# Feed-forward parts of 6 plain, 8 and 8 seven-product chunks, operands made in four steps, first turn of a part outside the weight ring

## The chip, the cores and the metric

The kernel runs on one core of a Trainium2 chip. Its time is the device time of one execution in microseconds (us); lower is better. TensorE (PE) multiplies, VectorE (DVE), ScalarE (ACT) and GpSimd (POOL) do the elementwise work, and SyncE (SP) issues nearly all DMAs. Each engine takes its instructions in the order in which they stand in its queue, and an instruction that waits holds up all behind it.

## The reference

A decoder trunk of two layers on 512 tokens of width 1024, in float32. Layer 0 is a convolution module, layer 1 differential attention. After each comes a SwiGLU feed-forward block of inner width 2816, which is what this change touches, and then a gated embedding:

```
h = h + conformer_conv(rms_norm(h))          # layer 0; layer 1: diff_attention
u = rms_norm(h, ffn_norm_g)
h = h + (silu(u @ w_gate) * (u @ w_up)) @ w_down
h = h + sigmoid(rms_norm(h, ple_norm_g) @ w) * (p @ w_proj)
```

## The kernel before

Activations lie transposed: a chunk is 128 features by 512 tokens, so h is 8 chunks and the inner width 22. Every float32 factor is split in two float32r parts, hi (a cast on ACT) and lo (a subtraction on DVE), and a product is three matmuls (`mm3`, L165 to L167): lo by hi, hi by hi, hi by lo.

**Weights.** `weight()` loads a tile of 128x1024 (SP) into a ring `wraw` of two buffers, casts it into a ring `whi` of four (ACT, L158) and subtracts into a ring `wlo` of four (DVE, L160). A ring slot comes free when the last matmul that reads it has ended.

**The feed-forward block**, `ffn()`, runs in three parts of 8, 8 and 6 inner chunks. Each part makes its hidden chunks (gate, up, silu, product, split into hi and lo in B tiles) and then runs its piece of the down-projection, `linear()`: for each of 8 output chunks m, one weight tile and as many `mm3` as the part has chunks, added to h by DVE (L885). Outputs 0 and 1 are computed together.

Hidden chunks are made in two ways. **Plain:** 24 matmuls of 512 columns each for gate and for up. **Seven-product:** two chunks at once. The input and the weights are taken as 2x2 blocks and the four block products come from seven, each of 12 matmuls of 256 columns, on sums and differences of blocks. One such turn (a `Unit`: Gate, then Up) needs, for its weights, six steps of `prep`: step 0 splits A11 and A12, steps 1 and 3 form sums on POOL (L721, L722, L726, L727), step 2 splits S1 and S2, step 4 splits S3 (L730, L731), step 5 splits S4 and A22. Steps 0, 2 and 5 each take a slot of `whi` and `wlo` (`two()`, L711, L712). For its input side it needs, once a layer, the operands of `operands()`: for four pairs of chunks, two scaled chunks u (DVE, L663), B11 (L666, L667), B21 and B22 (L670, L671), four differences T1 to T4 (POOL, L675 to L678) and their split (L680, L681).

In part one, 4 chunks are plain and 4 are seven-product; parts two and three are all seven-product. `operands()` stands in the program behind plain chunk 0, and the `prep` of part one's first turn behind plain chunk 3. The first turn of a later part is loaded and prepared by `begin()`, which `linear()` calls ahead of the weight of output chunk 6 of the part before. A Unit's result of its first product leaves PSUM by an ACT copy (L754), and product 6 then accumulates into the same PSUM half.

The order on each engine is set by a scheduler at build time, which moves instructions by its own estimate of times, within the program's dependences.

## Time and profile before

| | |
|---|---|
| median of 3 runs | 1311.98 us (1310.57 to 1314.16) |
| the profiled execution: its time | 1314.42 us |
| the profiled execution: its span, first to last instruction | 1312.6 us |
| PE busy | 1254.8 us, 96% |
| DVE busy | 890.8 us, 68% |
| ACT busy | 634.5 us, 48% |
| POOL busy | 537.4 us, 41% |

A busy PE is not a PE at full rate: a matmul's record includes the time it spends in the pipeline, and records overlap. The rate is read from the number of matmuls that start in a stretch. The column PEclk of a window is the share of full clock that TensorE was granted in it.

### The profile page before, as it was taken

To read this page: it belongs to the slowest core of one execution; us is meant where nothing else is said; L and a number is where in the kernel's file an instruction comes from. 1 tells how busy PE (TensorE), PEld (TensorE's weight loads), DVE (VectorE), ACT (ScalarE), POOL (GpSimd) and SP (SyncE) were. 2 spreads that over 40 slices of the span, in tenths; PEclk is the share of its full clock that TensorE was granted. 3 is DMA by queue.
4 is the path that set the end of the run, shared out by engine and by line. 5 is a ranking of instruction groups with operands and counts; after the bars stand their busy time and mean duration, and the time that the engine had idled before them with its cause. 6 is when DMAs were issued, how large, how long until landed. Compare 5 with 4: busy or idle time off the path is not lost.

```text
span 1312.6 us, 18775 instructions
## 1 busy us (share of the span) xinstructions
PE 1254.8 (96%) x7224; PEld 1099.4 (84%) x7224; DVE 890.8 (68%) x1208; ACT 634.5 (48%) x1116; POOL 537.4 (41%) x403
## 2 busy tenths in 40 slices
PE   9999999799899989999999999999699899989998
PEld 8888788698699869988888887888597799879987
DVE  6997957885279627666676876557874388438565
ACT  6643545453155315454666877644352255225342
POOL 3863523751347024223346635233930375036030
PEclk9999999889899989999999999999799899999999
DMA  7556232323133322234432330332233233322251
GB/s 262 193 185 184 65 97 80 97 88 121 49 99 111 105 72 86 73 111 144 129 117 86 106 98 9 95 114 80 82 100 109 67 108 99 98 74 71 73 152 64
DMA packets 49157, 136.37 MB, mean 104 GB/s; under 512 B 5635, under 2 KB 10243, under 8 KB 49068
## 3 DMA queue, kind: packets, MB, share of 16 engines
q1 hardware_dynamic: 46944, 131.74, 32.3%
q10 hardware_dynamic: 2124, 3.43, 0.9%
q8 instruction: 57, 0.93, 0.3%
q14 instruction: 32, 0.26, 0.1%
HBM read 128.84 MB, written 6.31 MB: 103 GB/s over the span
## 4 chain that ended last, share of the span: by engine, by line
PE 77%; DVE 8%; issue 3%; POOL 3%; DMA 2%; ACT 1%; SPq 0%; POOLq 0%; DVEq 0%; ACTq 0%
PE mm L165 24%; PE mm L166 23%; PE mm L167 23%; DVE wlo L160 2%; DVE wlo L712 1%; PE mm L1121 1%; DMA wraw<-in_wts 1%; DVE sc L448 1%; PE sc L1089 1%; PE sc L1088 1%; PE tp L1108 1%; ACT whi L158 1%; PE sc L397 1%; PE mm L397 1%; DVE B L663 1%
## 5 line engine op out<-in xcount | busy, mean ns | idle before, releaser
L158 ACT CAST whi<-wraw 128x1024 fp32r<-128x1024 f32 (+2 forms) x137 | 137.0, 1010 | 201.5 <-PE mm L167 142.8
L160 DVE TENSOR_TENSOR wlo<-wraw,whi 128x1024 fp32r<-128x1024 f32 (+2 forms) x133 | 175.7, 1327 | 63.8 <-ACT whi L158 63.6
L165 PE MATMUL mm<-A,wlo 128*128 128x512 f32 (+1 forms) x504 | 197.2, 392 | 0.1
L166 PE MATMUL mm<-A,whi 128*128 128x512 f32 (+1 forms) x504 | 194.6, 387 | 0.0
L167 PE MATMUL mm<-A,whi 128*128 128x512 f32 (+1 forms) x504 | 192.5, 389 | 0.0
L165 PE MATMUL mm<-C,wlo 128*128 128x256 f32 x540 | 154.3, 286 | 18.7 <-ACT big L754 18.7
L165 PE MATMUL mm<-B,wlo 128*128 128x512 f32 x352 | 143.4, 407 | 21.8 <-DVE wlo L160 21.8
L166 PE MATMUL mm<-C,whi 128*128 128x256 f32 x540 | 153.9, 285 | 0.0
L167 PE MATMUL mm<-C,whi 128*128 128x256 f32 x540 | 153.8, 285 | 0.0
L166 PE MATMUL mm<-B,whi 128*128 128x512 f32 x352 | 141.5, 402 | 0.0
L167 PE MATMUL mm<-B,whi 128*128 128x512 f32 x352 | 139.6, 401 | 0.0
L228 POOL TENSOR_TENSOR acc<-acc,wk 128x512 f32<-128x512 f32 x35 | 57.3, 1639 | 179.7 <-ACT wk L227 179.0
L712 DVE TENSOR_TENSOR wlo<-A,whi 128x1024 fp32r<-128x1024 f32 x70 | 113.1, 1622 | 16.5 <-ACT whi L711 16.3
L165 PEld LDWEIGHTS mm<-C,wlo 128*128 128x128 f32 x540 | 104.5, 194 | 19.6 <-ACT big L754 19.3
L165 PEld LDWEIGHTS mm<-A,wlo 128*128 128x128 f32 x504 | 94.8, 188 | 20.7 <-issue 1.4
L721 POOL TENSOR_TENSOR A<-A 128x512 f32<-128x512 f32 x18 | 28.1, 1560 | 205.3 <-DMA A<-in_wts 200.1
L166 PEld LDWEIGHTS mm<-A,whi 128*128 128x128 f32 x504 | 94.9, 188 | 19.5 <-issue 1.0
L167 PEld LDWEIGHTS mm<-A,whi 128*128 128x128 f32 x504 | 94.5, 188 | 19.5 <-issue 0.5
L885 DVE TENSOR_TENSOR h<-mm,h 128x512 f32<-128x512 f32 x48 | 33.0, 688 | 108.3 <-PE mm L167 108.3
L166 PEld LDWEIGHTS mm<-C,whi 128*128 128x128 f32 x540 | 104.7, 194 | 0.2
L167 PEld LDWEIGHTS mm<-C,whi 128*128 128x128 f32 x540 | 104.7, 194 | 0.0
L711 ACT CAST whi<-A 128x1024 fp32r<-128x1024 f32 x70 | 73.2, 1048 | 62.5 <-PE mm L167 52.9
(315 smaller groups left out, 3153.6 us busy)
## 6 DMA issues: line engine op xcount, KB each, us to landing
wraw<-in_wts SPq DMA_DIRECT2D x157, 512.0 KB, 3.6
A<-in_wts SPq DMA_DIRECT2D x36, 512.0 KB, 3.6
wraw<-in_wts SPq DMA_DIRECT2D x16, 384.0 KB, 3.0
D<-in_diag SPq DMA_DIRECT2D x22, 256.0 KB, 4.5
C<-in_diag SPq DMA_DIRECT2D x16, 256.0 KB, 4.7
h<-in_xT SPq DMA_DIRECT2D x8, 256.0 KB, 5.3
rest<-h SPq DMA_DIRECT2D x8, 256.0 KB, 2.7
bias<-scr ACTq DMA_DIRECT2D x8, 256.0 KB, 3.5
```

Source lines behind the costliest of these rows:

```text
L158: A.copy(hi[:, cut], raw[:, cut])
L160: eng.tensor_tensor(lo[:, cut], raw[:, cut], f(hi[:, cut]), ALU.subtract)
L165: T.matmul(acc, al, bh, start=first, stop=False, **kw)
L166: T.matmul(acc, ah, bh, start=False, stop=False, **kw)
L167: return T.matmul(acc, ah, bl, start=False, stop=last, **kw)
L228: self.last = self.eng.tensor_tensor(self.acc, self.acc, sq, ALU.add)
L397: last_tap[0] = T.matmul(acc[:, g * P : (g + 1) * P], w, ups[c][:, g, LEAD - m : LEAD - m + P], start=(m == 0), stop=(m == LAGS - 1),)
L448: last_v_tap[0] = V.scalar_tensor_tensor(sum_, tap(j), wt(c, j), sum_, ALU.mult, ALU.add)
L711: A.copy(hi, src)
L712: V.tensor_tensor(lo, src, f(hi), ALU.subtract)
L721: G.tensor_tensor(s[:, 0], r1[:, 0], r1[:, 1], ALU.add)
L885: V.tensor_tensor(h[m], acc, h[m], ALU.add)
```

## The change

The parts become 6, 8 and 8 chunks; part one is all plain, parts two and three are all seven-product. So each layer has 6 plain chunks instead of 4 and 16 seven-product turns (Units) instead of 18. The operands are made in four steps of one pair each, which stand behind plain chunks 1, 2, 4 and 5, use one u tile and one T tile in turn, and form T1 to T4 on DVE instead of POOL. The first turn of a part always stands in the down-projection of the part before: its raw tiles go to A0 and A1 and are loaded at output chunk 5, POOL's sums stand at chunk 6 (steps 1 and 3), the splits at chunk 7 (steps 0, 2, 4 and 5), and each hook is called behind the weight of its output chunk. Its S1 and S2 go to four `wk` tiles instead of a slot of `whi` and `wlo`; `Unit.first` now means the first turn of any part.

```diff
@@ -27,7 +27,7 @@
 KW = 31
 DFF = 2816
 FC = DFF // P
-PARTS = [(0, 8), (8, 8), (16, 6)]
+PARTS = [(0, 6), (6, 8), (14, 8)]
 EPS = 1e-6
 LAMBDA_INIT = 0.8 - 0.6 * math.exp(-0.3 * 1)
 NEG = -1.0e30
@@ -78,7 +78,8 @@
 LT = 2
 LA = 4
 PACK = True
-PLAIN = 4
+OPS_AT = (1, 2, 4, 5)
+HOOKS = {5: (None,), 6: (1, 3), 7: (0, 2, 4, 5)}
 HT = S // 2
 E1 = True
 GLO = 1
@@ -613,13 +614,13 @@
         m = 0
         while m < NC:
             g = group0 if m == 0 else 1
-            if m in at:
-                at[m]()
             ws = [
                 given[m + i] if m + i in given
                 else weight(n_in * P, after=split.get(m + i, (None, None)), home=home if m + i == 2 else None)
                 for i in range(g)
             ]
+            if m in at:
+                at[m]()
             accs = [mm() for _ in range(g)]
             for k in range(n_in):
                 if before:
@@ -648,40 +649,42 @@
         tags = ("wth", "wtl") if j == 0 else ("bias", "bias")
         return [sb([P, 2, HT], t, 2, F32R) for t in tags]
 
-    def operands(norm, rb, spare):
-
-        ub = [sb([P, 2, S], f"B{4 + j}", 1) for j in range(4)]
-        u = [ub[c // 2][:, c % 2] for c in range(NC)]
-        tops, uppers, lowers = spare()
-        low = []
-        for j in range(2):
-            lh, ll = lowers(j)
-            low += [(lh[:, i], ll[:, i]) for i in range(2)]
-        ops = {n: [None] * 4 for n in ("B11", "B21", "B22", "T1", "T2", "T3", "T4")}
-        for k in range(4):
-            for c in (k, k + 4):
-                V.scalar_tensor_tensor(u[c], h[c], col(norm.g, c), rb, ALU.mult, ALU.mult)
-            (u11, u12), (u21, u22) = ((u[c][:, :HT], u[c][:, HT:]) for c in (k, k + 4))
-            hi, lo = low[k]
-            A.copy(hi, u11)
-            V.tensor_tensor(lo, u11, f(hi), ALU.subtract)
-            ops["B11"][k] = hi, lo
-            hi, lo = uppers(k)
-            A.copy(hi, u[k + 4])
-            V.tensor_tensor(lo, u[k + 4], f(hi), ALU.subtract)
-            ops["B21"][k] = hi[:, :HT], lo[:, :HT]
-            ops["B22"][k] = hi[:, HT:], lo[:, HT:]
-            t = sb([P, 4, HT], f"B{2 + k % 2}", 1)
-            G.tensor_tensor(t[:, 0], u12, u11, ALU.subtract)
-            G.tensor_tensor(t[:, 1], u22, t[:, 0], ALU.subtract)
-            G.tensor_tensor(t[:, 2], u22, u12, ALU.subtract)
-            G.tensor_tensor(t[:, 3], u21, t[:, 1], ALU.subtract)
-            hi, lo = tops(k)
+    class Operands:
+
+        def __init__(self, norm, spare):
+            self.norm = norm
+            self.tops, self.uppers, lowers = spare()
+            self.low = []
+            for j in range(2):
+                lh, ll = lowers(j)
+                self.low += [(lh[:, i], ll[:, i]) for i in range(2)]
+            self.at = {n: [None] * 4 for n in ("B11", "B21", "B22", "T1", "T2", "T3", "T4")}
+
+        def chunk(self, k, rb):
+            ub = sb([P, 2, S], "B6", 1)
+            u1, u2 = both(ub)
+            for c, u in ((k, u1), (k + 4, u2)):
+                V.scalar_tensor_tensor(u, h[c], col(self.norm.g, c), rb, ALU.mult, ALU.mult)
+            (u11, u12), (u21, u22) = ((u[:, :HT], u[:, HT:]) for u in (u1, u2))
+            hi1, lo1 = self.low[k]
+            A.copy(hi1, u11)
+            hi2, lo2 = self.uppers(k)
+            A.copy(hi2, u2)
+            t = sb([P, 4, HT], "B7", 1)
+            V.tensor_tensor(t[:, 0], u12, u11, ALU.subtract)
+            V.tensor_tensor(t[:, 1], u22, t[:, 0], ALU.subtract)
+            V.tensor_tensor(t[:, 2], u22, u12, ALU.subtract)
+            V.tensor_tensor(t[:, 3], u21, t[:, 1], ALU.subtract)
+            hi, lo = self.tops(k)
             A.copy(hi, t)
+            V.tensor_tensor(lo1, u11, f(hi1), ALU.subtract)
+            self.at["B11"][k] = hi1, lo1
+            V.tensor_tensor(lo2, u2, f(hi2), ALU.subtract)
+            self.at["B21"][k] = hi2[:, :HT], lo2[:, :HT]
+            self.at["B22"][k] = hi2[:, HT:], lo2[:, HT:]
             V.tensor_tensor(lo, t, f(hi), ALU.subtract)
             for i in range(4):
-                ops[f"T{i + 1}"][k] = hi[:, i], lo[:, i]
-        return ops
+                self.at[f"T{i + 1}"][k] = hi[:, i], lo[:, i]
 
     class Unit:
 
@@ -699,12 +702,8 @@
                 raw = sb([P, 2, S], *(("wraw", 2) if self.raws == "wraw" else (f"A{j}", 1)))
                 nc.sync.dma_start(raw, wts[self.i + j].rearrange("p (j k) -> p j k", j=2))
                 self.raw.append(raw)
-            if self.first:
-                self.sums = sb([P, 2, S], "B6", 1)
-                self.s3 = wk()
-            else:
-                self.sums = sb([P, 2, S], f"A{2 + self.n % 2}", 1)
-                self.s3 = sb([P, 2, S], f"A{6 + self.n % 2}", 1)[:, 0]
+            self.sums = sb([P, 2, S], f"A{2 + self.n % 2}", 1)
+            self.s3 = sb([P, 2, S], f"A{6 + self.n % 2}", 1)[:, 0]
 
         def two(self, src, a, b):
             hi, lo = sb([P, 2, S], "whi", 4, F32R), sb([P, 2, S], "wlo", 4, F32R)
@@ -721,12 +720,19 @@
                 G.tensor_tensor(s[:, 0], r1[:, 0], r1[:, 1], ALU.add)
                 G.tensor_tensor(s[:, 1], s[:, 0], r0[:, 0], ALU.subtract)
             elif step == 2:
-                self.two(s, "S1", "S2")
+                if self.first:
+                    for j in range(2):
+                        hi, lo = wk(F32R), wk(F32R)
+                        A.copy(hi, s[:, j])
+                        V.tensor_tensor(lo, s[:, j], f(hi), ALU.subtract)
+                        self.w[f"S{j + 1}"] = hi, lo
+                else:
+                    self.two(s, "S1", "S2")
             elif step == 3:
                 G.tensor_tensor(s3, r0[:, 0], r1[:, 0], ALU.subtract)
                 G.tensor_tensor(r1[:, 0], r0[:, 1], s[:, 1], ALU.subtract)
             elif step == 4:
-                hi, lo = both(sb([P, 2, S], "B7" if self.first else f"A{4 + self.n % 2}", 1, F32R))
+                hi, lo = both(sb([P, 2, S], f"A{4 + self.n % 2}", 1, F32R))
                 A.copy(hi, s3)
                 V.tensor_tensor(lo, s3, f(hi), ALU.subtract)
                 self.w["S3"] = hi, lo
@@ -798,26 +804,18 @@
 
     def ffn(norm, after, spare):
         rb = None
-        ops = None
-        early = []
-
-        def units(at, f0, n, hid):
+        ops = Operands(norm, spare)
+
+        def units(n, hid):
             us = []
-            for i in range(f0, n, 2):
-                k = len(us)
-                raws = "wraw" if k % 2 == (0 if at == 0 else 1) else "A"
-                g = Gate(k, at == 0 and k == 0, raws)
-                u = Up(k + 1, False, "A" if raws == "wraw" else "wraw")
+            for i in range(0, n, 2):
+                g, u = Gate(2 * (i // 2), i == 0, "A"), Up(2 * (i // 2) + 1, False, "wraw")
+                g.hid = hid
                 u.gate, u.at, u.hid = g, i, hid
                 us += [g, u]
             for x in us:
-                x.b = ops
+                x.b = ops.at
             return us
-
-        def begin(us):
-            us[0].load()
-            for step in range(6):
-                us[0].prep(step)
 
         def run(us):
             for n, x in enumerate(us):
@@ -849,12 +847,14 @@
             us[-1].p(4)
             us[-1].p(3)
 
+        us = None
         for at, (f0, n) in enumerate(PARTS):
-            if at == 0:
-                hid = [None] * n
+            if us:
+                run(us)
+                hid = us[0].hid
             else:
-                hid = hid2
-            for i in range(PLAIN if at == 0 else 0):
+                hid = []
+            for i in range(0 if us else n):
                 wg, wu = weight(), weight()
                 pg, pu = mm(), mm()
                 for k in range(NC):
@@ -873,13 +873,9 @@
                 hl = sb([P, 2, S], f"B{i}", 1, F32R)
                 A.copy(hl[:, 0], tu)
                 V.tensor_tensor(hl[:, 1], tu, f(hl[:, 0]), ALU.subtract)
-                hid[i] = (hl[:, 0], hl[:, 1])
-                if i == 0:
-                    ops = operands(norm, rb, spare)
-            if at == 0:
-                us = units(at, PLAIN, n, hid)
-                begin(us)
-            run(us)
+                hid.append((hl[:, 0], hl[:, 1]))
+                if i in OPS_AT:
+                    ops.chunk(OPS_AT.index(i), rb)
 
             def add(m, acc):
                 V.tensor_tensor(h[m], acc, h[m], ALU.add)
@@ -891,15 +887,15 @@
                 n2 = PARTS[at + 1][1]
                 now = wnext[0]
                 wnext[0] += NC
-                hid2 = [None] * n2
-                us2 = units(at + 1, 0, n2, hid2)
+                us = units(n2, [None] * n2)
                 end = wnext[0]
                 wnext[0] = now
-                hooks[6] = lambda: begin(us2)
+                x = us[0]
+                for m, steps in HOOKS.items():
+                    hooks[m] = partial(lambda steps: [x.load() if k is None else x.prep(k) for k in steps], steps)
             linear(n, hid, add, 2, at=hooks)
-            if at < len(PARTS) - 1:
+            if hooks:
                 wnext[0] = end
-                us = us2
 
     def ple(norm, pp, after, last_cuts=1):
         def sums(m, cuts=1):
@@ -1317,7 +1313,7 @@
         g, u = _stationary(a["ffn_w_gate"][i]), _stationary(a["ffn_w_up"][i])
         r = []
         for f0, n in PARTS:
-            plain = PLAIN if f0 == 0 else 0
+            plain = n if f0 == 0 else 0
             for c in range(f0, f0 + plain):
                 r += [g[c], u[c]]
             for c in range(f0 + plain, f0 + n, 2):
```

The scheduler's order shows what this does to the queues. First **DVE in layer 0, at the end of part one's down-projection**: L160 (L161 in the change) is the lo part of a down-projection weight, L712 (L711 in the change) the lo part of a turn's `two()`, L731 (L737) of S3, L885 (L881) the addition to h. Before, from the first split of part two's first turn (its raw tiles are A_486 and A_487, its sums A_488; h_10 to h_14 are output chunks 3 to 7):

```order
L712 TENSOR_TENSOR wlo_2832<-A_486_2825,whi_2831 128x1024
L885 TENSOR_TENSOR h_10_90<-mm_2735,h_10_90 128x512
L712 TENSOR_TENSOR wlo_2838<-A_488_2829,whi_2837 128x1024
L885 TENSOR_TENSOR h_11_91<-mm_2767,h_11_91 128x512
L712 TENSOR_TENSOR wlo_2847<-A_487_2827,whi_2846 128x1024
L885 TENSOR_TENSOR h_12_92<-mm_2799,h_12_92 128x512
L160 TENSOR_TENSOR wlo_2852<-wraw_2850,whi_2851 128x1024
L885 TENSOR_TENSOR h_13_93<-mm_2856,h_13_93 128x512
L160 TENSOR_TENSOR wlo_2884<-wraw_2882,whi_2883 128x1024
L885 TENSOR_TENSOR h_14_94<-mm_2888,h_14_94 128x512
```

In the change, the same place (raw tiles A_443 and A_444; the first two L161 are output chunks 6 and 7; A_470 and wraw_2512 are of the second turn):

```order
L161 TENSOR_TENSOR wlo_2437<-wraw_2435,whi_2436 128x768
L881 TENSOR_TENSOR h_10_90<-mm_2357,h_10_90 128x512
L161 TENSOR_TENSOR wlo_2467<-wraw_2465,whi_2466 128x768
L881 TENSOR_TENSOR h_11_91<-mm_2383,h_11_91 128x512
L711 TENSOR_TENSOR wlo_2472<-A_443_2409,whi_2471 128x1024
L737 TENSOR_TENSOR A_477_2584<-A_470_2517,A_477_2584 128x512
L881 TENSOR_TENSOR h_12_92<-mm_2415,h_12_92 128x512
L711 TENSOR_TENSOR wlo_2487<-A_444_2411,whi_2486 128x1024
L881 TENSOR_TENSOR h_13_93<-mm_2445,h_13_93 128x512
L711 TENSOR_TENSOR wlo_2534<-wraw_2512,whi_2533 128x1024
```

The two weights of output chunks 6 and 7 stood behind three splits of the coming turn and now stand ahead of all of them; S1 and S2 no longer appear among the splits there.

Next **ACT in layer 0, ahead of the first seven-product turn**. Before, L754 is the copy of that turn's first product out of PSUM, L711 and L730 are splits of turns, L680 the cast of T1 to T4, and L874 the hi part of a plain hidden chunk:

```order
L711 CAST whi_2143<-B_400_2135 128x1024
L680 CAST C_359_1898<-B_358_1893 128x1024
L711 CAST whi_2152<-wraw_2133 128x1024
L680 CAST C_363_1914<-B_362_1909 128x1024
L730 CAST B_406_2149<-wk_2136 128x512
L711 CAST whi_2179<-A_411_2158 128x1024
L874 CAST B_386_2057<-big_2052 128x512
L754 COPY big_2156<-mm_2164 128x256
```

In the change, at the step from the last plain chunk to the first down-projection, L159 is the cast of a down-projection weight (chunks 2 and 3, later 4, 5 and 6), L726 casts S1 and S2 into `wk` tiles, L736 casts S3, and L874 is the hi part of plain chunk 5:

```order
L159 CAST whi_2326<-wraw_2325 128x768
L870 ACTIVATE big_2247<-big_2247 128x512
L159 CAST whi_2352<-wraw_2351 128x768
L726 CAST wk_2475<-A_445_2413 128x512
L874 CAST B_414_2253<-big_2248 128x512
L736 CAST A_461_2483<-A_446_2414 128x512
L726 CAST wk_2479<-A_445_2413 128x512
L159 CAST whi_2378<-wraw_2377 128x768
L159 CAST whi_2404<-wraw_2403 128x768
L159 CAST whi_2436<-wraw_2435 128x768
```

The splits of turns and the casts of T that stood right ahead of the PSUM copy are gone from that place; S1 of the coming turn now stands ahead of the hi part of hidden chunk 5, and S3 and S2 ahead of the weights of output chunks 4 to 7.

Last **SP in the change, at the same place**: L155 loads a down-projection weight (output chunks 2 and 3 ahead, 4 and 5 behind), L703 the first turn's raw tiles.

```order
L155 DMA wraw_2325<-in_wts 128x768
L155 DMA wraw_2351<-in_wts 128x768
L703 DMA A_443_2409<-in_wts 128x1024
L703 DMA A_444_2411<-in_wts 128x1024
L155 DMA wraw_2377<-in_wts 128x768
L155 DMA wraw_2403<-in_wts 128x768
```

The raw tiles of part two's first turn are issued behind the weight of output chunk 3, and the weight of chunk 4 behind them.

## The prediction

> **What bounds the kernel now.** I read the page first, then who waits for whom on PE, then windows of each stage of the feed-forward blocks, then the timelines of ACT and DVE where PE stands.
>
> ```profile
> span 1312.6 us, 18775 instructions
> PE 1254.8 (96%) x7224; PEld 1099.4 (84%) x7224; DVE 890.8 (68%) x1208; ACT 634.5 (48%) x1116; POOL 537.4 (41%) x403
> ```
>
> PE is busy for 96% of the span, so time is gained only where PE stands or runs slowly, or by giving it fewer columns. Its waits are few (total, times, longest):
>
> ```profile
> PE mm L165 <- DVE wlo L160: 21.8, 8, 3.1
> PE mm L165 <- ACT big L754: 18.7, 3, 9.1
> PE mm L165 <- DVE wlo L712: 6.1, 5, 2.7
> ```
>
> Eight waits are for the lo part of a `weight()`, three for the copy of a turn's first product out of PSUM. What they cost in all is read from windows; x is the number of matmuls that touch the window:
>
> ```profile
> core 0: us, PE busy (x) PEld busy (x) DVE busy (x) ACT busy (x) POOL busy (x), PEclk, DMA share, GB/s
> 310.00:335.00 25.00, 25.00 (x111) 20.45 (x110) 10.93 (x12) 5.79 (x6) 0.00 (x0) 1.00 0.29 88
> 364.00:424.00 60.00, 60.00 (x503) 60.00 (x502) 49.88 (x53) 34.19 (x59) 37.33 (x22) 1.00 0.35 104
> 248.00:271.00 23.00, 11.23 (x62) 10.73 (x62) 18.92 (x13) 10.52 (x16) 22.84 (x16) 0.63 0.24 69
> 335.00:356.00 21.00, 15.58 (x55) 11.91 (x54) 4.47 (x4) 2.09 (x2) 6.64 (x5) 0.84 0.23 72
> 356.00:364.00 8.00, 7.00 (x55) 6.53 (x54) 5.50 (x5) 3.76 (x7) 4.76 (x4) 1.00 0.11 25
> 424.00:434.00 10.00, 9.71 (x81) 9.51 (x80) 9.48 (x10) 5.13 (x10) 5.40 (x3) 1.00 0.29 101
> 470.00:492.00 22.00, 16.49 (x57) 12.57 (x56) 4.83 (x5) 2.71 (x3) 9.51 (x7) 0.84 0.22 70
> 927.00:951.00 24.00, 12.23 (x71) 11.73 (x71) 19.58 (x13) 10.58 (x16) 23.84 (x16) 0.64 0.22 66
> 1014.00:1031.00 17.00, 11.59 (x38) 8.61 (x38) 4.46 (x4) 2.09 (x2) 5.99 (x4) 0.80 0.23 62
> 1100.00:1112.00 12.00, 11.61 (x97) 11.41 (x97) 10.79 (x12) 6.62 (x13) 7.53 (x4) 1.00 0.30 88
> 1148.00:1165.00 17.00, 11.58 (x42) 8.72 (x42) 4.47 (x4) 2.09 (x2) 6.01 (x4) 0.90 0.26 74
> ```
>
> The first two are undisturbed. Taking 1.5 from x for matmuls cut by the edges, a matmul of 512 columns starts every 25/109.5 = 0.228 us (a down-projection), one of 256 every 60/501.5 = 0.120 us (six turns of 84 each, 10.1 us a turn). For the others, the time lost is the length less (x - 1.5) times that pitch:
>
> - the first turn of part one, 248 and 927: 23 - 60.5 x 0.120 = 15.7, and 24 - 69.5 x 0.120 = 15.7; together **31.4**;
> - the ends of the down-projections of parts one and two (0.228): 21 - 12.2 = 8.8, 22 - 12.7 = 9.3, 17 - 8.3 = 8.7, 17 - 9.2 = 7.8; together **34.6**;
> - the start and end of part two (356, 424, 1100): 1.6, 0.5, 0.5; together **2.6**.
>
> Sum: 68.6 us. The lost time is more than the waits because the granted clock falls after each: 0.63 in the window at 248, where a wait of 9.1 became a loss of 15.7, a factor of 1.7.
>
> Why PE stands at 248:
>
> ```profile
> 251.00 1.04 ACT L711 CAST whi<-B 128x1024 fp32r<-128x1024 f32 x1 [4.44 <-POOL B L722]
> ...
> 256.24 1.04 ACT L680 CAST C<-B 128x1024 fp32r<-128x1024 f32 x1 [0.62 <-POOL B L678]
> ...
> 259.17 0.36 ACT L754 COPY big<-mm 128x256 f32<-128x256 f32 x1
> ```
>
> POOL still makes T and the turn's sums (22.84 of 23 us busy); ACT waits for it, and the PSUM copy for which PE waits is queued behind. Why it stands at 335:
>
> ```profile
> 336.79 1.04 ACT L158 CAST whi<-wraw 128x1024 fp32r<-128x1024 f32 x1 [4.40 <-PE mm L167]
> 348.28 1.04 ACT L158 CAST whi<-wraw 128x1024 fp32r<-128x1024 f32 x1 [10.44 <-PE mm L167]
> ```
>
> The coming turn holds three of the four `whi` slots, so the weights of output chunks 6 and 7 share the last: each is cast only when PE has finished the chunk before, and PE waits for cast and subtraction.
>
> **The change, part by part.** *Matmuls.* Per layer two turns (168 matmuls of 256) become two plain chunks (96 of 512): 96 x 0.228 - 168 x 0.120 = 21.9 - 20.2 = 1.7, so **+3.4** for both layers, all on PE's path. The down-projection keeps its 22 chunks. The Trainium skill (TensorE: Matmul & The Clock Gate, Back-to-back issue gap) gives an isolated gap of N/2.4 + 2.5 ns at full clock, 109 and 216 ns. By it the swap would cost 2.4 a layer, 4.7 in all, since its short matmuls keep their half price; this trace's 120 ns decides.
>
> *First turn of part one* (-31.4). No turn stands behind the plain chunks any more; six chunks and a down-projection lie between the first operand step and the first product. POOL's 16 differences a layer go to DVE:
>
> ```profile
> L675 POOL TENSOR_TENSOR B<-B 128x256 f32<-128x256 f32 x4 | 5.4, 1346 | 15.7 <-DVE B L663 9.1 <-DVE C L681 6.6
> L677 POOL TENSOR_TENSOR B<-B,B 128x256 f32<-128x256 f32 x4 | 6.1, 1522 | 0.0
> L663 DVE SCALAR_TENSOR_TENSOR B<-h,vec,rb 128x512 f32<-128x512 f32 x8 | 8.3, 1106 | 0.0
> L681 DVE TENSOR_TENSOR C<-B,C 128x1024 fp32r<-128x1024 f32 x2 | 2.4, 1211 | 0.0
> L160 DVE TENSOR_TENSOR wlo<-wraw,whi 128x1024 fp32r<-128x1024 f32 x2 | 2.4, 1208 | 0.0
> L671 DVE TENSOR_TENSOR C<-B,C 128x512 fp32r<-128x512 f32 x3 | 2.0, 678 | 0.0
> L667 DVE TENSOR_TENSOR bias<-B,bias 128x256 fp32r<-128x256 f32 x2 | 0.8, 412 | 0.0
> ```
>
> DVE has not done these differences; the row of the same size is L667 at 0.41, the bound above a contended POOL row, 1.5. I take 0.41, since both read two SBUF operands of 256 and POOL is idle there. One step on DVE is then 2 x 1.11 (upper, they ran beside POOL) + 4 x 0.41 + 0.41 + 0.68 + 1.21 = 6.2, and a plain chunk's own work is two L160 and four operations of 512 (as L671), 2 x 1.21 + 4 x 0.68 = 5.1: 11.3, against 48 x 0.228 = 10.9 of PE. At most 0.4 behind per chunk, for four chunks: 1.6. The cover is the ring of four: a weight can be cast from the end of the gate half two chunks earlier, so 2 x 10.9 - 5.5 - 1.05 - 1.21 = 14 us of slack. So nothing on the path; without that cover 1.6 a layer, 2.7 with the clock's factor.
>
> *Hooks in the down-projection* (-34.6). In the new order the weights of chunks 6 and 7 stand ahead of the turn's splits on ACT and DVE, and the turn needs two slots, not three, which are those of chunks 4 and 5. A chunk takes 18 x 0.228 = 4.1 us of PE, so the slot of chunk 4 is free 12 us before the turn begins, against 1.04 + 1.21 for a split. S1 and S2 need four `wk` tiles, which nobody holds there. Gone, then, for four transitions; were the cover of 12 us not there, they would cost what they do now.
>
> *What is late next.* In part one ACT has S1's cast (behind POOL, behind the DMA of A0 and A1) ahead of the hi part of hidden chunk 5, and DVE its lo part likewise; behind them stand the additions to h, which free PSUM. A1's old reader is the up half of chunk 5, so it is free about 4 us before the down-projection begins.
>
> ```profile
> L721 POOL TENSOR_TENSOR A<-A 128x512 f32<-128x512 f32 x18 | 28.1, 1560 | 205.3 <-DMA A<-in_wts 200.1
> A<-in_wts SPq DMA_DIRECT2D x36, 512.0 KB, 3.6
> ```
>
> Two transfers of 3.6 back to back land at +3.2 at the latest, at once in parallel at about 0; then 1.6 (L721), a cast of 0.6, chunk 5's own cast 0.6: +2.8 to +6.0. PE reaches chunk 5 after 30 matmuls, +6.8, and wants its lo part at about +7.7. I take no wait; the bound is two contended POOL operations more in the way, about 5 us late, 8.5 a layer with the clock's factor (**rival 1**).
>
> *The 2.6 at part starts and ends* stay; parts two and three are of the same kind. Bounds: 0 and twice that.
>
> Sum for the profiled execution: 1312.6 - 31.4 - 34.6 + 3.4 = 1250.0 of span. Its time was 1314.42, 1.8 over its span, so 1251.8; the median is 2.4 below that execution. **1249.4**, against 1312.0 before. The floor, with the 2.6 gone too, is 1246.8.
>
> **Rivals.**
> 1. *S1 takes the place of the weights* (above): two layers, up to 8.5 each, so 1258 to 1266. For it: the margin is 1 to 4 us, and SP has A0 and A1 ahead of chunk 4's weight. Against: the DMA rate in the window at 335 is 72 GB/s, so the queue is not full.
> 2. *The ring still binds:* the turn's two slots and the next turn's first make the last weights late as before. The four transitions keep 34.6: 1284. For it: four buffers are still four. Against: the order has both weights ahead of every split.
> 3. *Slower: DVE bounds the plain chunks.* If DVE and ACT work in turn and not side by side (each split waits for its cast, each cast for its u or T), a chunk takes DVE's 11.3 and ACT's share:
>
> ```profile
> L680 ACT CAST C<-B 128x1024 fp32r<-128x1024 f32 x4 | 4.2, 1048 | 1.6 <-POOL B L678 1.6
> L870 ACT ACTIVATE big<-big 128x512 f32<-128x512 f32 x4 | 2.5, 630 | 7.8 <-DVE big L869 7.8
> 337.87 1.86 DVE L160 TENSOR_TENSOR wlo<-wraw,whi 128x1024 fp32r<-128x1024 f32 x1 [0.38 <-ACT whi L158]
> ```
>
> three casts of 1.05, three operations of 0.63 and one of 0.4 make 5.4, and five hand-overs of 0.38 make 1.9: 18.6 a chunk. Five chunks then come 5 x (18.6 - 10.9) - 14 = 24.5 late, 42 with the clock's factor, 83 for two layers: 1249 + 83 = 1332, slower by 1.5%. It decides from the chunk time at which this eats 62.6: (62.6/2/1.7 + 14)/5 + 10.9 = 17.4 us. For it: DVE is filled to 11.3 of 10.9. Against: in the new order other work stands between a cast and its subtraction almost everywhere, and 14 us of slack come first. The Trainium skill (Perfetto Trace Analysis, Optimizing Scalar/DVE Operations) says that where DVE is saturated, work may better go to ScalarE or even GpSimd, with the caution that the latter shares a port with DVE; by it this change moves work the wrong way, and this rival is what it would give. The rows speak for its caution: the same difference took 1.35 to 1.52 us on POOL.
>
> That the change doesn't do what it says needs the scheduler to move the hooks back; the order shows that it did not for the weights, and rival 1 is what it did with S1.
>
> **Chances.** Forecast 75%, with its own range 1246 to 1257; rival 1 15%; rival 2 6%; rival 3 4%. The range of 8 in 10 goes from 1245, the floor less the runs' spread, to 1264, most of rival 1. A change under 0.3% (4 us) can't be told from none here: faster 0.95, same 0.01, slower 0.04.
>
> **What would show it.** Right: PE's waits for L754 and for the weights' lo part gone from the list; PEclk 1.00 through the plain chunks and the down-projections; a plain chunk at 10.9 us; DVE near full from plain chunk 1 to 4, and no wait of PE there. Rival 1 shows as a wait in the middle of the first down-projection of a layer, on B's hi or lo part; rival 2 as PE waits for a weight's lo part at the end of each down-projection; rival 3 as waits for a weight's lo part in the plain chunks with PEclk below 1. I am wrong if PE's waits shrink and the time does not, or if the waits move to a stage that I call untouched (convolution, attention, embedding: the same rows in the same order).

## The result, and the profile after

The changed kernel takes 1250.14 us (median, 1248.59 to 1251.6) beside 1311.28 (1310.57 to 1314.16) of the kernel before: a ratio of 0.953, with a 95% interval of 0.951 to 0.9549. Forecast were 1249.4 us, and faster. The profiled execution took 1249.66 us, with a span of 1247.6, 65.0 less than before.

The top of the page of the changed kernel, and its clock in 40 slices of the span (9 is 90% or more):

```profile
span 1247.6 us, 18420 instructions
PE 1236.4 (99%) x7080; PEld 1081.5 (87%) x7080; DVE 877.6 (70%) x1230; ACT 623.0 (50%) x1096; POOL 470.5 (38%) x355
PEclk9999999999999999999999999999999999999999
```

PE is busy for 99% instead of 96%, though its busy time is 18 us less. Who waits for whom on PE, the first rows of that view (us in total, times, longest):

```profile
PE tp L141 <- POOL ident masks.py:199: 1.5, 1, 1.5
PE sc L398 <- DMA C<-pi: 1.3, 1, 1.3
PE sc L1084 <- DVE st L1087: 1.3, 2, 1.0
PE tp L589 <- ACT wk L586: 0.7, 1, 0.7
PE tp L1147 <- ACT wtl L1106: 0.6, 1, 0.6
PE mm L166 <- DVE big L768: 0.4, 1, 0.4
```

The three rows that made 46.6 us before (the PSUM copy, and the lo parts of weights and of turns) are gone. All that is left of the feed-forward blocks is one wait of 0.4; the first five rows belong to the start, the convolution and attention. Windows of the first feed-forward block of the changed kernel (columns as in the prediction's table):

```profile
220.00:242.00 22.00, 22.00 (x99) 18.20 (x98) 21.61 (x35) 12.01 (x18) 0.00 (x0) 1.00 0.31 94
242.00:285.00 43.00, 43.00 (x191) 35.63 (x190) 33.29 (x45) 16.53 (x23) 6.57 (x4) 1.00 0.31 100
304.00:364.00 60.00, 60.00 (x503) 59.99 (x502) 48.81 (x51) 33.26 (x57) 38.53 (x23) 1.00 0.31 92
364.00:376.00 12.00, 11.64 (x98) 11.44 (x97) 11.28 (x12) 5.14 (x10) 8.64 (x5) 1.00 0.29 82
```

With the prediction's pitches (0.228 us for a matmul of 512 columns, 0.120 for 256) and 1.5 taken from each count, the first is two chunks' worth of plain matmuls with operand steps beside them (the middle of plain chunk 1 to the middle of 3): 97.5 x 0.228 = 22.2 of 22. The second goes from there into the down-projection: 189.5 x 0.228 = 43.2 of 43. The third, six turns, is full as it was before (60.2 of 60). The fourth is the end of part two: 12 - 96.5 x 0.120 = 0.4 lost. DVE is 98% busy in the first window, and PE waits for nothing there.

To count what PE lost over whole blocks, I added, over all pairs of neighbouring matmuls of the feed-forward blocks, the time between two starts beyond the pitch of the first: 36.4 and 34.1 us in the two layers before, 1.1 and 0.9 after. So 68.5 us of lost time are gone, and the matmuls cost 3.4 more by their pitches; what is left of the gain, 65.1, is what the span fell by (65.0).

### The profile page after: what moved, and what is told of

Same layout as the page of the kernel before. It is cut to its first block, busy times and chain, and to the rows that moved or that the text cites. A ratio compares the mean times of both kernels' runs of the same rounds, so it can differ in the third digit from the quotient of the medians.

```text
span 1247.6 us, 18420 instructions
## 1 busy us (share of the span) xinstructions
PE 1236.4 (99%) x7080; PEld 1081.5 (87%) x7080; DVE 877.6 (70%) x1230; ACT 623.0 (50%) x1096; POOL 470.5 (38%) x355
## 4 chain that ended last, share of the span: by engine, by line
PE 88%; DVE 5%; issue 2%; DMA 1%; ACT 1%; SPq 0%; POOL 0%; DVEq 0%; ACTq 0%
PE mm L166 27%; PE mm L167 27%; PE mm L168 27%; PE mm L1117 1%; DVE sc L449 1%; DVE wlo L161 1%; PE sc L1085 1%; PE sc L1084 1%; PE tp L1104 1%; PE sc L398 1%; PE mm L398 1%; PE tp L1038 1%; PE mm L354 1%; PE tp L199 1%; DVE wlo L711 0%
## 5 line engine op out<-in xcount | busy, mean ns | idle before, releaser
L159 ACT CAST whi<-wraw 128x1024 fp32r<-128x1024 f32 (+2 forms) x145 | 145.6, 1013 | 220.2 <-PE mm L168 97.2
L161 DVE TENSOR_TENSOR wlo<-wraw,whi 128x1024 fp32r<-128x1024 f32 (+2 forms) x141 | 179.3, 1277 | 73.7 <-ACT whi L159 73.5
L166 PE MATMUL mm<-A,wlo 128*128 128x512 f32 (+1 forms) x568 | 222.5, 392 | 0.3 <-ACT A L206 0.2
L167 PE MATMUL mm<-A,whi 128*128 128x512 f32 (+1 forms) x568 | 219.8, 388 | 0.0
L168 PE MATMUL mm<-A,whi 128*128 128x512 f32 (+1 forms) x568 | 217.6, 389 | 0.0
L166 PEld LDWEIGHTS mm<-A,wlo 128*128 128x128 f32 x568 | 106.9, 188 | 23.6 <-issue 1.4
L167 PE MATMUL mm<-C,whi 128*128 128x256 f32 x448 | 127.0, 283 | 0.0
L168 PE MATMUL mm<-C,whi 128*128 128x256 f32 x448 | 127.0, 283 | 0.0
L166 PE MATMUL mm<-C,wlo 128*128 128x256 f32 x448 | 127.0, 283 | 0.0
L167 PEld LDWEIGHTS mm<-A,whi 128*128 128x128 f32 x568 | 107.0, 188 | 22.0 <-issue 1.0
L168 PEld LDWEIGHTS mm<-A,whi 128*128 128x128 f32 x568 | 106.6, 188 | 21.9 <-issue 0.5
L711 DVE TENSOR_TENSOR wlo<-A,whi 128x1024 fp32r<-128x1024 f32 x60 | 104.6, 1752 | 21.0 <-ACT whi L710 21.0
L710 ACT CAST whi<-A 128x1024 fp32r<-128x1024 f32 x60 | 62.9, 1048 | 56.6 <-PE mm L168 45.3
L720 POOL TENSOR_TENSOR A<-wraw 128x512 f32<-128x512 f32 x16 | 25.4, 1589 | 170.3 <-DMA wraw<-in_wts 156.1
L720 POOL TENSOR_TENSOR A<-A 128x512 f32<-128x512 f32 x16 | 25.3, 1581 | 161.9 <-DMA A<-in_wts 159.2
L167 PEld LDWEIGHTS mm<-C,whi 128*128 128x128 f32 x448 | 86.1, 192 | 0.2
L166 PEld LDWEIGHTS mm<-C,wlo 128*128 128x128 f32 x448 | 86.1, 192 | 0.2
L168 PEld LDWEIGHTS mm<-C,whi 128*128 128x128 f32 x448 | 86.1, 192 | 0.0
```

The lines of the kernel that those rows point to most:

```text
L159: A.copy(hi[:, cut], raw[:, cut])
L161: eng.tensor_tensor(lo[:, cut], raw[:, cut], f(hi[:, cut]), ALU.subtract)
L166: T.matmul(acc, al, bh, start=first, stop=False, **kw)
L167: T.matmul(acc, ah, bh, start=False, stop=False, **kw)
L168: return T.matmul(acc, ah, bl, start=False, stop=last, **kw)
L710: A.copy(hi, src)
```

## The experiments

Times are medians; a ratio is against the kernel before, measured on the same chip, with its 95% interval. "Lost" is counted as just said.

### The hooks alone, on the kernel before

The parts, the operands and part one's first turn stay as before. Only the later parts' first turns get the new hooks.

```diff
+HOOKS = {5: (None,), 6: (1, 3), 7: (0, 2, 4, 5)}
...
-            if m in at:
-                at[m]()
             ws = [
...
             ]
+            if m in at:
+                at[m]()
...
-                self.two(s, "S1", "S2")
+                if self.apart:
+                    for j in range(2):
+                        hi, lo = wk(F32R), wk(F32R)
...
+                g.apart, u.apart = at > 0 and k == 0, False
...
-                hooks[6] = lambda: begin(us2)
+                x = us2[0]
+                for m, steps in HOOKS.items():
+                    hooks[m] = partial(lambda steps: [x.load() if k is None else x.prep(k) for k in steps], steps)
```

> The kernel before with the hooks of the down-projection alone changed: the weight of an output chunk ahead of the hook, the six steps spread over output chunks 5, 6 and 7, and S1 and S2 of the first turn of parts two and three in wk tiles. My sum: the 34.6 us at the four ends of down-projections go and nothing else does: 1311.3 - 34.6 = 1276.7. If the terms overlap (the first turn's stall moves something there) it is not additive: 1285 or more.

Measured: 1277.3 us (1276.84 to 1278.36), ratio 0.9744 [0.9725, 0.9763] beside 1311.37. PE's first waits in this kernel:

```profile
PE mm L166 <- ACT big L762: 18.2, 2, 9.1
PE mm L166 <- DVE wlo L713: 5.3, 2, 2.7
```

The eight waits at the ends of down-projections are gone and those at part one's first turn untouched (L762 and L713 are L754 and L712 of before), with 16.0 and 15.3 us lost around them. The gain is 34.1, against 34.6 in the sum. The rest of the change then brings 1277.3 - 1250.1 = 27.2, against 31.4 - 3.4 = 28.0. The two parts add.

### Which part of the hooks does it

The hooks do two things: they put the weights of output chunks 6 and 7 ahead of the turn's splits, and they keep S1 and S2 out of the ring, so that the turn takes two slots and not three. Three runs on the changed kernel take back both, the second alone, and the first alone.

Both:

```diff
-HOOKS = {5: (None,), 6: (1, 3), 7: (0, 2, 4, 5)}
+HOOKS = {6: (None, 0, 1, 2, 3, 4, 5)}
...
+            if m in at:
+                at[m]()
             ws = [
...
-            if m in at:
-                at[m]()
             accs = [mm() for _ in range(g)]
...
-                if self.first:
+                if False:
```

> The change with the old hooks: all six steps ahead of the weight of output chunk 6, S1 and S2 of the first turn in the ring. My sum: the 34.6 us come back, 1250.1 + 34.6 = 1284.7, with PE waiting for a weight's lo part at each end of a down-projection. If the longer parts gave cover of their own: 1250 to 1260.

S1 and S2 in the ring, the order as in the change (only the last line of that diff):

> The change with S1 and S2 of a first turn back in the ring (three slots), hooks behind the weights as in the change. If what cost the time was that three slots of four are held AND taken ahead of the last two weights, the order alone repairs it: 1250. If the third slot alone is the cause (the prediction's rival 2 read strictly): PE waits at the start of the turn, up to 1284.

The order as before, S1 and S2 in `wk` (all of that diff but its last line):

> The change with all six steps ahead of the weight of output chunk 6, but S1 and S2 in wk tiles (two slots). The weights of chunks 6 and 7 then use the slots of chunks 4 and 5, each free one chunk (4.1 or 5.5 us) before it is needed, against a cast and a subtraction of about 2.6: 1250 to 1252 by my theory. If the order alone is the cause: as with the old hooks, 1284.

| | order of before | order of the change |
|---|---|---|
| S1, S2 in the ring (three slots) | 1281.71, 0.9774 [0.9751, 0.9797] | 1249.56, 0.953 [0.9511, 0.9549] |
| S1, S2 in `wk` (two slots) | 1250.35, 0.954 [0.9519, 0.9561] | 1250.14, 0.953 [0.951, 0.9549] |

Either repair is enough alone; the loss needs both faults together. PE's first wait in the run with both, and what ACT does at that end of the down-projection (L159 casts a weight, L710 casts for a turn):

```profile
PE mm L166 <- DVE wlo L161: 18.7, 8, 3.1
```

```profile
289.69 1.05 ACT L710 CAST whi<-A 128x1024 fp32r<-128x1024 f32 x1 [3.03 <-PE mm L168]
293.73 0.83 ACT L159 CAST whi<-wraw 128x768 fp32r<-128x768 f32 x1 [2.98 <-PE mm L168]
301.62 0.83 ACT L159 CAST whi<-wraw 128x768 fp32r<-128x768 f32 x1 [7.06 <-PE mm L168]
```

It is the picture of before: the weights of chunks 6 and 7 come from one slot, each cast when PE has ended a chunk. The waits of 18.7 cost 1281.71 - 1250.14 = 31.6 us. With two slots for the turn, two are left for the last two weights, and the order no longer matters; with the weights ahead, it no longer matters how many the turn takes after them.

### The engine that makes T1 to T4

In the changed kernel with its cover, and alone in the kernel before, where no cover is:

```diff
-            V.tensor_tensor(t[:, 0], u12, u11, ALU.subtract)
-            V.tensor_tensor(t[:, 1], u22, t[:, 0], ALU.subtract)
-            V.tensor_tensor(t[:, 2], u22, u12, ALU.subtract)
-            V.tensor_tensor(t[:, 3], u21, t[:, 1], ALU.subtract)
+            G.tensor_tensor(t[:, 0], u12, u11, ALU.subtract)
+            G.tensor_tensor(t[:, 1], u22, t[:, 0], ALU.subtract)
+            G.tensor_tensor(t[:, 2], u22, u12, ALU.subtract)
+            G.tensor_tensor(t[:, 3], u21, t[:, 1], ALU.subtract)
```

> The change with the 16 differences T1 to T4 of a layer back on POOL, at four operand steps as in the change. POOL needs about 4 x 1.3 = 5.3 us a step, once per plain chunk of 10.9, so the steps keep pace and six chunks and a down-projection of cover remain: 1250 by my theory (where the differences are made is worth nothing once there is cover). If POOL's slowness itself was the cause of the first turn's stall: PE waits again ahead of part two, up to 1281.

Measured: 1249.77 us (1248.97 to 1251.69), ratio 0.9521 [0.9503, 0.954]. The same window, 220 to 242, of that run:

```profile
220.00:242.00 22.00, 22.00 (x99) 18.20 (x98) 19.86 (x26) 11.83 (x17) 10.66 (x9) 1.00 0.23 72
```

POOL works 10.66 us there, and DVE is little relieved (19.86 against 21.61), but PE starts the same 99 matmuls. The other way round, T on DVE in the kernel before (the same lines with + and - exchanged, in `operands()`):

> The kernel before with T1 to T4 on DVE and nothing else. If the cover (four plain chunks, with DVE at 21.8 of 22 us) is what lacked, part of the stall of 15.7 a layer stays: I expect about half, 1311.3 - 16 = 1295. If POOL alone was the cause, the 31.4 go: 1280. If DVE is simply too full, no change or slower: 1311 to 1320.

Measured: 1305.61 us (1305.05 to 1306.12), ratio 0.9944 [0.9927, 0.9962] beside 1313.55.

```profile
PE mm L165 <- DVE wlo L160: 21.7, 8, 3.2
PE mm L165 <- DVE wlo L712: 14.4, 4, 4.3
```

```profile
248.00:284.00 36.00, 28.16 (x204) 27.23 (x203) 33.10 (x37) 18.15 (x30) 21.78 (x12) 0.86 0.24 74
```

T is off POOL, and PE now waits at part one's first turn for the splits on DVE (L712). Of 15.8 us lost there in layer 0, 36 - 202.5 x 0.120 = 11.7 stay in this window, and about as much in layer 1. So taking T off POOL, with the load that it puts on DVE, is worth the 7.9 us of time that this run gained, a quarter of the 31.4; I had put it at half. The rest is work for a turn that comes too late for it, on either engine. It goes when six chunks and a down-projection lie ahead of the turn: the run before had that with T on POOL, and lost nothing there. How much of that cover is needed, and whether the four separate operand steps matter in it, was not tried apart on six chunks.

### More plain chunks

Parts of 8, 8 and 6 with part one all plain: two more plain chunks and two turns less a layer, at the same pitches.

```diff
-PARTS = [(0, 6), (6, 8), (14, 8)]
+PARTS = [(0, 8), (8, 8), (16, 6)]
```

> The change with parts of 8 plain, 8 and 6 seven-product chunks: two more turns a layer become plain. My price for the swap of matmuls, 1.7 a layer, gives 1250.1 + 3.4 = 1253.5. By an isolated gap of 109 and 216 ns it would be 4.7: 1254.8.

Measured: 1253.57 us (1253.12 to 1254.79), ratio 0.955 [0.9532, 0.9567]: 3.4 above the change, as the pitches of the trace have it, 1.7 for two chunks of a layer. An estimate by the isolated gap of the Trainium skill (TensorE: Matmul & The Clock Gate, Back-to-back issue gap) would be 4.7. With runs that spread over 1.7 and 3.0 us the time alone doesn't tell 3.4 from 4.7; what speaks against the gap here is the pitch itself, 0.228 and 0.120 us in the traces for 0.216 and 0.109.

### Fewer plain chunks, where the prediction's cover ends

Parts of 4, 6, 6 and 6 should gain those 3.4 again, if the operands are still ready. They leave a down-projection of 12 matmuls a chunk, 2.7 us instead of 4.1, which shortens the cover for everything in it.

```diff
-PARTS = [(0, 6), (6, 8), (14, 8)]
+PARTS = [(0, 4), (4, 6), (10, 6), (16, 6)]
...
-OPS_AT = (1, 2, 4, 5)
+OPS_AT = (0, 1, 2, 3)
```

> Parts of 4 plain, 6, 6 and 6 seven-product chunks, an operand step behind each plain chunk. By matmuls alone the swap goes the other way: 1250.1 - 3.4 = 1246.7. But S1 of the first turn then stands ahead of the hi part of hidden chunk 4, which PE wants after 18 matmuls (4.1 us) and not after 30, so about 3 to 4 us late in each layer, with the clock's factor 6 a layer: 1259. Part of the operand steps is also later than the plain chunks.

Measured: 1260.93 us (1259.66 to 1262.6), ratio 0.9601 [0.958, 0.9622]; 8.0 us a layer lost in the first down-projection. (Layer 1's projection reads its weights at a wrong offset in this run, since the count of weights assumes three parts; the work is the same.) PE's first waits:

```profile
PE mm L166 <- DVE wlo L161: 7.5, 2, 3.7
PE mm L168 <- DVE B L875: 1.8, 2, 0.9
```

The larger is the lo part of an output chunk's weight, the smaller that of a hidden chunk: the place that rival 1 named. I took S1 and T's load on DVE as its causes and took each away, and both: T on POOL and S1, S2 in the ring; T on DVE and the ring; T on POOL and `wk`.

```diff
-PROJ1 = 16 + 2 + 8 + 2 * FC + 3 * NC + 8 + 4 * len(QKV)
+PROJ1 = 16 + 2 + 8 + 2 * FC + len(PARTS) * NC + 8 + 4 * len(QKV)
...
-            V.tensor_tensor(t[:, 0], u12, u11, ALU.subtract)
+            G.tensor_tensor(t[:, 0], u12, u11, ALU.subtract)
...
-                if self.first:
+                if False:
```

> Parts of 4 plain, 6, 6 and 6 seven-product chunks with T1 to T4 on POOL and S1 and S2 of the first turns in the ring, so that neither stands ahead of the last hidden chunk or of the down-projection's weights on DVE. PE lost 8 us a layer in the run of 4, 6, 6 and 6 before; if these two are the cause, 1260.9 - 16 = 1245, faster than the change by the swap of matmuls (3.4) and a little. If four plain chunks are simply too little cover: 1250 to 1260. The projection of layer 1 takes its own weights here (the run before took them from a wrong offset, which counts three parts; the work is the same).

> The same parts, T1 to T4 on DVE, S1 and S2 in the ring. If S1's place ahead of the hidden chunk was the cause (rival 1): 1246. If DVE's load of T1 to T4 was: 1257 to 1260.

> The same parts, T1 to T4 on POOL, S1 and S2 in wk tiles. If DVE's load of T1 to T4 was the cause: 1246. If S1's place was (rival 1): 1255 to 1260.

Measured: 1261.93 (ratio 0.9614 [0.9591, 0.9636]), 1263.26 (0.9623 [0.9597, 0.9649]) and 1261.97 us (0.9619 [0.9594, 0.9643]). None is better, so neither cause was one that counted. In the run with both taken away one long wait is left, 4.9 us a layer, for the weight of output chunk 4. POOL, ACT and DVE ahead of it, and PE's windows there:

```profile
249.29 2.06 POOL L674 TENSOR_TENSOR B<-B 128x256 f32<-128x256 f32 x1 [3.86 <-DVE C L685]
253.81 1.74 POOL L720 TENSOR_TENSOR A<-A 128x512 f32<-128x512 f32 x1
255.51 1.28 POOL L732 TENSOR_TENSOR A<-A,A 128x512 f32<-128x512 f32 x1
```

```profile
256.82 0.62 ACT L736 CAST A<-A 128x512 fp32r<-128x512 f32 x1 [3.62 <-POOL A L732]
257.52 1.05 ACT L679 CAST C<-B 128x1024 fp32r<-128x1024 f32 x1
258.47 1.13 ACT L159 CAST whi<-wraw 128x512 fp32r<-128x512 f32 x2
```

```profile
257.48 1.80 DVE L737 TENSOR_TENSOR A<-A,A 128x512 fp32r<-128x512 f32 x1 [3.08 <-ACT A L736]
259.20 2.28 DVE L685 TENSOR_TENSOR C<-B,C 128x1024 fp32r<-128x1024 f32 x1
261.41 1.28 DVE L881 TENSOR_TENSOR h<-mm,h 128x512 f32<-128x512 f32 x2
262.61 0.68 DVE L161 TENSOR_TENSOR wlo<-wraw,whi 128x512 fp32r<-128x512 f32 x1
```

```profile
258.00:262.80 4.80, 0.45 (x2) 0.03 (x1) 4.80 (x5) 1.61 (x3) 2.32 (x2) 1.00 0.00 0
262.80:266.00 3.20, 2.66 (x7) 2.13 (x8) 2.28 (x4) 0.01 (x1) 0.00 (x0) 0.64 0.36 90
```

Read backwards: the weight's subtraction (L161, 262.61) stands behind the split of the last T (L685) and that of S3 (L737), these behind their casts on ACT, and S3's cast behind POOL, which makes three of the fourth operand step's differences (from L674 at 249.29 to 253.85) ahead of the turn's sums (L720, L732). The scheduler puts that step, the turn's steps and the weights one behind the other into the first 16 us (247.4 to 263.3) of a down-projection of 22. The last run leaves the fourth step out (the turns use the third step's operands in its place).

```diff
-                if i in OPS_AT:
-                    ops.chunk(OPS_AT.index(i), rb)
+                if i in OPS_AT[:3]:
+                    ops.chunk(i, rb)
+            if not us:
+                for p in ops.at.values():
+                    p[3] = p[2]
```

> The kernel with parts of 4, 6, 6 and 6 chunks, T1 to T4 on POOL and S1, S2 in the ring, without the fourth operand step: the turns use the third step's operands in its place, so the output is not the reference's, and PE's work is the same. In the kernel with the fourth step POOL made that step's T1 to T4 from 249.3 to 253.8, then the turn's sums until 256.8; the splits of S3 and of T followed on ACT and DVE, and only then the weight of output chunk 4, for which PE stood 4.9 us a layer. Theory: the fourth step, packed into a part of four chunks, is what is late. Then the sums end some 4 us sooner, the weight of chunk 4 is split before PE wants it, the waits for a weight's lo part fall from 9.8 to under 2, and with the clock's factor the time falls by 10 to 16, to 1246 to 1252. Rival: the turn's sums and splits, or the loads behind them, are late by themselves in a down-projection of 22 us; then 3 us or more a layer of the wait stay and the time is 1256 to 1262.

Measured: 1249.47 us (1248.27 to 1249.75), ratio 0.9515 [0.9491, 0.954]; no wait for L161 is left on PE's list. POOL and DVE at the same place (L884 is L881):

```profile
248.89 1.29 POOL L720 TENSOR_TENSOR A<-A 128x512 f32<-128x512 f32 x1 [3.26 <-DMA A<-in_wts]
250.14 1.74 POOL L732 TENSOR_TENSOR A<-A,A 128x512 f32<-128x512 f32 x1
```

```profile
247.89 0.68 DVE L161 TENSOR_TENSOR wlo<-wraw,whi 128x512 fp32r<-128x512 f32 x1
249.10 1.64 DVE L161 TENSOR_TENSOR wlo<-wraw,whi 128x512 fp32r<-128x512 f32 x1
254.05 1.77 DVE L737 TENSOR_TENSOR A<-A,A 128x512 fp32r<-128x512 f32 x1
255.75 1.27 DVE L884 TENSOR_TENSOR h<-mm,h 128x512 f32<-128x512 f32 x2
256.95 0.68 DVE L161 TENSOR_TENSOR wlo<-wraw,whi 128x512 fp32r<-128x512 f32 x1
```

Without the step S3's sum starts 5.4 us sooner (250.14 against 255.51), and chunk 4's weight is split 5.7 us sooner, in time. The fourth step behind the last plain chunk is what was late in this version, not S1. Even without that step a part of four plain chunks gains nothing here: counted as above, 5.4 us are still lost in its blocks, against 2.0 in the change, which eats the 3.4 of cheaper matmuls. Which of that step's pieces weighs most, POOL's differences or the splits, was not tried apart, and for the other three versions the chain was not followed to its end.

None of these versions beats the change by more than the intervals allow: S1 and S2 in the ring (1249.56) and T on POOL (1249.77) are the same as it, 1250.14.

## Why the prediction was right, point by point

**The 31.4 at part one's first turn** and **the 34.6 at the ends of down-projections** went as forecast, at the places forecast. The hooks alone brought 34.1, the rest 27.2 where 28.0 were due. What the prediction did not see is that the 34.6 had two sufficient repairs; it listed both as reasons ("ahead of the turn's splits", "two slots, not three") and treated them as one. **Rival 2**, that four buffers are still four, falls with the same runs: with three slots and the new order the time is 1249.56, not 1284.

**The matmul swap, +3.4.** Not seen apart in the change itself; the run with eight plain chunks repeats it, and its median is 3.4 higher, within the spread of the runs.

**Operand steps on DVE at no cost.** Right, and nearly at the edge: DVE is 21.61 us busy of 22.00. The disputed prices are now measured (least, median and greatest, ns):

```profile
L674 DVE TENSOR_TENSOR B<-B x8: 416/419/425, 225.2 to 901.4; 128x256 f32<-128x256 f32 x8
L667 DVE SCALAR_TENSOR_TENSOR B<-h,vec,rb x16: 742/747/752, 222.1 to 897.8; 128x512 f32<-128x512 f32 x16
```

A difference took 0.42, where 0.41 was taken from the row of the same size; the scaled chunk 0.75, where 1.11 was an upper bound. So a chunk with a step is 11.3 - 2 x 0.36 = 10.6 us of DVE, under PE's 10.9, and **rival 3** had less ground than it was given. Moving the work to POOL instead, because DVE is full, is neither better nor worse here: 1249.77 with T on POOL.

**What is late next: rival 1.** It did not happen, but its margin was smaller than the prediction's 1 to 4 us. Its place in the changed kernel, on ACT and on DVE (the down-projection starts at 269.19; L874 and L875 make hidden chunk 5's hi and lo):

```profile
271.20 0.62 ACT L726 CAST wk<-A 128x512 fp32r<-128x512 f32 x1 [0.92 <-POOL A L720]
271.75 0.62 ACT L874 CAST B<-big 128x512 fp32r<-128x512 f32 x1
```

```profile
273.60 1.77 DVE L727 TENSOR_TENSOR wk<-A,wk 128x512 fp32r<-128x512 f32 x1
275.30 1.77 DVE L875 TENSOR_TENSOR B<-big,B 128x512 fp32r<-128x512 f32 x1
277.00 0.68 DVE L737 TENSOR_TENSOR A<-A,A 128x512 fp32r<-128x512 f32 x1
```

The hi part ends at +3.2, near the lower end of the estimate (+2.8 to +6.0). The lo part ends at 277.07, +7.9: S1's split stands ahead of it, and both took 1.77 us beside POOL instead of 0.68, which the estimate for DVE left out. PE wants it 36 matmuls after the start, at +8.2 and not at +7.7, because the scheduler let it begin output chunk 2 first. So 0.3 us were left.

**The clock's factor of 1.7 was misread.** The prediction took it from the window at 248 as a loss of 15.7 for one wait of 9.1. PE waits twice in that window of the kernel before:

```profile
259.59 0.58 PE L165 MATMUL mm<-C,wlo 128*128 128x256 f32 x1 [9.10 <-ACT big L754]
265.19 0.58 PE L165 MATMUL mm<-wth,wlo 128*128 128x256 f32 x1 [2.67 <-DVE wlo L712]
```

11.8 us of waits became 15.7, a factor of 1.3. The forecast does not use the factor, but the prices of rivals 1 and 3 do; over the waits of these runs it goes from 1.3 to 1.7. The second wait is for a split on DVE (L712), the kind that stayed with T on DVE.

**The term that failed is "the 2.6 at part starts and ends stay".** 0.8 stay: by single gaps, 0.5 and 0.3 at the end of part two in the two layers. The starts of parts now cost nothing, though the prediction called parts two and three "of the same kind" as before. It was the hooks that did this: the run with them alone loses nothing at the starts of parts either, and 0.6 and 0.4 at the end of part two.

That miss and another cancel. **The last step, "the median is 2.4 below that execution", does not carry over.** The seven executions of the kernel before that were timed beside the last three runs with 4, 6, 6 and 6 chunks and all their work go from 1308.58 us at a granted clock of 0.984 to 1315.69 at 0.977; I take what varies to be what its waits cost. The changed kernel has no such waits, and its executions stay at 0.998 to 1.000. So nothing had to be taken off for it: 1312.6 - 31.4 - 34.6 + 3.4, with 0.8 for 2.6, is 1248.2 of span, and the 2.1 to 2.2 by which the times of its executions exceed their spans make 1250.3, beside a median of 1250.14. That the forecast came within 0.7 us is luck in so far as these two misses, 1.8 too high and 2.4 too low, cancel. In this account the mechanism is shown, the split of these last 2 us only argued.

**Where the working was wrong without being tested by the result:** the share of POOL in the first turn's loss, which only the run with T on DVE in the kernel before showed; the clock's factor; and the cause of rival 1, which in a shorter down-projection turned out to be the last operand step and not S1, in the one version whose chain was followed to its end.

## What to carry to other kernels

Where a rotating buffer runs dry at the end of a stage, count for each claimant both how many slots it takes and whether it stands ahead of the last users in the queue: either one may repair it, and the cheaper can be chosen. Work that must be ready for a stage is bought with distance, not with a faster engine: moving it alone brought 8 us, moving the stage away from it 27. Before a stage is shortened, look at what was packed into its cover; here a down-projection of chunks of 2.7 us instead of 4.1 turned no wait at all into 8 us of loss a layer.

## What the runs showed of the hardware

A DVE subtraction of two SBUF operands of 128x512 took 0.68 us with POOL idle and 1.64 to 1.80 where it came behind a POOL operation (the rows at 247.89 and 249.10 in the run without the fourth step show it within 1.3 us, as POOL starts at 248.89). The Trainium skill (SBUF — State Buffer, SBUF: two separate sides) says that such a DVE operation and a POOL operation that reads SBUF take turns whole, the loser fully blocked. The rows agree: L161, issued at 249.10, ends at 250.74, 0.56 after POOL's L720 (248.89 + 1.29 = 250.18), about its own 0.68 behind it. This is what the estimate of rival 1's margin lacked: twice 1.77 for 0.68, 2.2 us. DVE is not always the one that waits. In the four-chunk run with both causes taken away it was POOL:

```profile
249.46 0.69 DVE L161 TENSOR_TENSOR wlo<-wraw,whi 128x512 fp32r<-128x512 f32 x1
253.11 0.74 POOL L675 TENSOR_TENSOR B<-B,B 128x256 f32<-128x256 f32 x1
```

The subtraction took 0.69 there, and POOL's L674, which ran beside it from 249.29, took 2.06 for a difference of the size that L675 made in 0.74.

The clock's price differs from wait to wait. Waits of 18.7 us in all, none over 3.1, cost 31.6 (1.7 times, by the medians) at the ends of down-projections; the waits of 9.1 and 2.7 at the turn cost 1.3 times. After the wait of 4.9 in that four-chunk run the granted clock was 0.64 for 3.2 us, and 1.7 us were lost there in layer 0 and 2.9 in layer 1 beyond the wait itself (1.3 and 1.6 times). The changed kernel, with no wait of PE over 1.5, ran at 0.999.
